# The keys' low parts of the attention logits as two zero-padded 128-row tiles in place of one tile read by halves

## The chip, the cores and the metric

The kernel runs on one core of a Trainium2 chip. The metric is the device time of one execution in microseconds (us), lower is better. The core has five engines that each run their own list of instructions in order: TensorE (PE in the profile, its weight loads as PEld), VectorE (DVE), ScalarE (ACT), GpSimd (POOL) and SyncE (SP), which here issues the transfers.

## What is computed

Two transformer layers, one after the other, on 512 tokens of width 1024 in float32. The first has sliding-window attention with a sink, differential attention and a convolutional feed-forward block. The second has sparse latent attention (an index score picks the keys), a gated linear recurrence and a merge of both. The change touches one kind of product, the logits of queries against keys in heads of 64, which the reference has in four places:

```python
HEAD_DIM = 64
# swa_sink_attention, WINDOW = 128: a block of 128 queries against 256 keys
scores = jnp.einsum("bnqhgd,bnkhd->bnhgqk", qb, kk).astype(jnp.float32)
scores = scores * (HEAD_DIM ** -0.5)
# diff_attention, Q_BLOCK = 128: 4 heads of 2 maps, against all earlier keys
s = jnp.einsum("bqhmd,bkhmd->bhmqk", q_blk, k).astype(jnp.float32)
# sparse_mla_attention: index scores of 8 heads, then the logits of 16 heads
s_idx = jax.nn.relu(jnp.einsum('btjd,bsd->btjs', qi.astype(f32), k_idx_f))
s_idx = jnp.einsum('btjs,btj->bts', s_idx, wi.astype(f32))
_, idx = lax.top_k(s_idx, topk)
logits = jnp.einsum('bthc,btkc->bthk', ql.astype(f32), c_sel)
```

## The kernel before

All activations lie transposed, features on the 128 partitions and the 512 tokens along the free dimension. A projection ("unit") is a 1024 x 128 piece of a weight matrix: eight contraction steps, and in each three matmuls of 512 columns, because every float32 operand is split into a high part (type fp32r, one pass through TensorE) and a low part that holds the rest: high times high, high times low, low times high (`mm3`, lines 534 to 546). The weights come by DMA into `wr`; ACT makes their high part `wh`, and POOL or DVE the low part `wl` (`hi_w`, `lo_w`, lines 477 to 511). Where the four `wh` buffers are taken, the two parts go into ordinary slots and are named `sh` and `sl`.

The logits take heads in pairs, e = 0 and 1, on partitions 0 to 63 and 64 to 127. The query tile `sq` of each e (`stack_q`, lines 614 to 631) holds the high part in its own 64 partitions and the low part in the other 64. The key tile `sk` of each e (`stack_k`, lines 633 to 647) holds the high part twice, so one matmul over 128 rows gives high times high plus low times high. What is left, query high times key low, comes from one more tile `skl`, whose lower half belongs to e = 0 and upper half to e = 1. `logits` (lines 649 to 659) issues four matmuls per block of 128 queries: two over 128 rows (`sk`) and two over 64 rows (`skl`), the latter on the upper and on the lower half of TensorE's array; the results are accumulated in two banks `ps_lg`. They have 256, 384 or 512 columns, by how many keys the block sees.

`stack_k` makes its tiles with two ACT copies (`sk`), two DVE copies of 64 partitions (`sk<-sk`, CAST in the profile) and two DVE subtractions (`skl`). It is called 14 times: once for the windowed keys (`ka`), four times for the differential keys (`kb0` to `kb3`), once for the index keys (`kn`) and eight times in the last attention stage, there straight from the bank in which the pair's keys were projected (`ev_q`, lines 1705 to 1719). `logits` is called 76 times: 32 in the first layer (47 to 177 us: 24 of 256 columns, 4 of 384, 4 of 512), 12 in the index scores (850 to 930 us: 4 of each width), 32 in the last attention stage (1040 to 1205 us: 16, 8 and 8).

The order of all instructions is settled while the program is built. The projections are issued in a fixed list, and between their contraction steps a planner (`sched`, lines 437 to 451) lets the other jobs, written as generators, emit their next piece as soon as its clock for each engine says that the inputs are there. `account` (lines 288 to 355) moves these clocks by a price per instruction. `vp` (lines 357 to 360) gives an elementwise job to POOL or to DVE, whichever clock is earlier. So an instruction added to one engine can move others:

```python
elif key == "P":
    c = 0.15 + n * 0.0021
p = max(self.free["P"], now) + PRM["pe"] + bias
return self.nc.gpsimd if p < max(self.free["D"], now) else self.nc.vector
```

Intermediate tiles come from one pool of 52 slots of 128 x 512 float32 (`slot`, line 266). A new tile waits for the last readers of the slot that it gets.

Of the kernel before, what the change touches and what calls it, by code (L numbers as in the profile page):

```python
# [12 lines left out]
F32 = mybir.dt.float32  # L13
F32R = mybir.dt.float32r
# [219 lines left out]
class _Build:  # L234
# [189 lines left out]
    def ok(self, g):  # L424
# [3 lines left out]
        if h == "T":  # L428
            return g.ready <= now + PRM["lt"]
        if h == "L":  # L430
            return self.cur >= UIDX[PRM["tk"]] and max(g.ready, self.free["D"]) <= now + PRM["ll"]
# [182 lines left out]
    def stack_q(self, src, scale=None):  # L614
        nc = self.nc
        A = [self.slot("sq0", F32R), self.slot("sq1", F32R)]
        R = (slice(0, 64), slice(64, 128))
        for e in range(2):
            yield "A"
            if scale is None:  # L620
                nc.scalar.activation(A[e][R[e], :], src[R[e], :], AF.Copy)
            else:
                nc.scalar.activation(A[e][R[e], :], src[R[e], :], AF.Identity, scale=scale[R[e], :])
        for e in range(2):
            yield "D"
            if scale is None:
                nc.vector.tensor_sub(A[e][R[1 - e], :], src[R[e], :], A[e][R[e], :].bitcast(F32))
                continue
            nc.vector.scalar_tensor_tensor(A[e][R[1 - e], :], src[R[e], :], scale[R[e], :],
                                           A[e][R[e], :].bitcast(F32), op0=OP.mult, op1=OP.subtract)  # L630
        return A

    def stack_k(self, src):
        nc = self.nc
        B = [self.slot("sk0", F32R), self.slot("sk1", F32R)]
        L = self.slot("skl", F32R)
        R = (slice(0, 64), slice(64, 128))
        for e in range(2):
            yield "A"
            nc.scalar.activation(B[e][R[e], :], src[R[e], :], AF.Copy)  # L640
        for e in range(2):
            yield "D"
            nc.vector.tensor_copy(B[e][R[1 - e], :], B[e][R[e], :])
        for e in range(2):
            yield "D"
            nc.vector.tensor_sub(L[R[e], :], src[R[e], :], B[e][R[e], :].bitcast(F32))
        return B, L

    def logits(self, pls, q, k, b, c0, c1, o=0):
        nc = self.nc  # L650
        if c1 - c0 < 256:
            c1 = c0 + 256
        B, L = k
        w = slice(b * P, (b + 1) * P)
        for e in range(2):
            nc.tensor.matmul(pls[e][:, o:o + c1 - c0], q[e][:, w], B[e][:, c0:c1], start=True, stop=False)
        for e in range(2):
            r = slice(64 * e, 64 * e + 64)
            nc.tensor.matmul(pls[e][:, o:o + c1 - c0], q[e][r, w], L[r, c0:c1], start=False, stop=True)

    def new_xs(self):
        out = []
# [157 lines left out]
    def block1(self):  # L820
# [68 lines left out]
        def swa(b):  # L889
# [3 lines left out]
            for gp in range(2):  # L893
# [3 lines left out]
                for g in (0, 1):  # L897
                    self.logits(pls, T[f"qa{2 * gp + g}"], T["ka"], b, c0, c0 + 256, g * 256)
                Lp = [self.slot("L"), self.slot("L")]
                for g in (0, 1):  # L900
# [1044 lines left out]
```

## Time and profile before

| | |
|---|---|
| three runs | 1345.79, 1349.64, 1350.53 us; median 1349.64 us |
| span of the profiled execution (first to last instruction) | 1344.5 us |
| PE busy | 1305.5 us, 97% of the span, 6748 matmuls |
| DVE, ACT, POOL busy | 903.1, 706.9, 286.8 us (67%, 53%, 21%) |
| bytes moved | 113.23 MB, mean 84 GB/s |

The page gives the profiled execution's span, and no time of its own beside it; the three runs are 1.3 to 6.0 us longer than that span, the median 5.1 us. A matmul's busy time is modelled and overlaps the next one's, so what a stretch costs PE is read from the starts of the instructions. Nearly every row has line 214, that of a helper which records each instruction; rows are told apart by the names of the tiles (output <- inputs), and "64\*128" beside a matmul means that it uses 64 of the array's 128 rows.

### The profile page before, as it was taken

How to read it: one execution, taken by the hardware profiler on the slowest of the kernel's cores; microseconds unless marked ns; L12 is line 12 of the kernel's file. 1: busy time of each engine (PE TensorE's matmuls, PEld its weight loads, DVE VectorE, ACT ScalarE, POOL GpSimd, SP SyncE). 2: the span in 40 equal slices, each digit the busy share in tenths (PEclk: the TensorE clock that was granted, in tenths of full speed). 3: DMA queues.
4: the chain of work that ended last, by engine and by line, in shares of the span. 5: the costliest groups of instructions: out<-in, count | busy, mean ns of one | idle time of the engine just before them, and what ended most of it. 6: DMA issues, size and time to landing. Idle time of an engine off the chain costs nothing.

```text
span 1344.5 us, 17797 instructions
## 1 busy us (share of the span) xinstructions
PE 1305.5 (97%) x6748; PEld 1052.4 (78%) x6748; DVE 903.1 (67%) x1586; ACT 706.9 (53%) x1256; POOL 286.8 (21%) x176
## 2 busy tenths in 40 slices
PE   9999998999999999999999888999999999999997
PEld 6778888788888888888887876777788777777886
DVE  6767768877266736673677698588989667653354
ACT  6488675443234323441335447778772777773232
POOL 3200014323033303430343353031220000000111
PEclk9999999999999999999999998999999999999999
DMA  6212231132323332223324310222233121112221
GB/s 231 79 33 63 63 126 48 63 94 94 98 90 94 94 110 83 90 95 110 94 82 138 126 48 1 94 78 78 79 99 105 48 63 48 51 52 89 97 74 63
DMA packets 34245, 113.23 MB, mean 84 GB/s; under 512 B 3824, under 2 KB 5872, under 8 KB 34160
## 3 DMA queue, kind: packets, MB, share of 16 engines
q1 hardware_dynamic: 32192, 109.48, 25.2%
q10 hardware_dynamic: 1968, 2.62, 0.6%
q8 instruction: 53, 0.87, 0.3%
q14 instruction: 32, 0.26, 0.1%
HBM read 109.99 MB, written 2.10 MB: 83 GB/s over the span
## 4 chain that ended last, share of the span: by engine, by line
PE 80%; DVE 12%; ACT 4%; issue 1%; DMA 1%; POOL 0%; ACTq 0%; SPq 0%; DVEq 0%; POOLq 0%
PE ps_mm L214 61%; PE ps_lg L214 9%; PE ps_o L214 8%; PE ps_pt L214 3%; DVE c L214 3%; DVE sl L214 1%; DVE xl L214 1%; DVE sq L214 1%; ACT c L214 1%; ACT wh L214 1%; ACT L214 1%; DVE yo L214 1%; DVE score L214 1%; DVE fs L214 0%; ACT sq L214 0%
## 5 line engine op out<-in xcount | busy, mean ns | idle before, releaser
L214 PE MATMUL ps_mm<-xh,wh 128*128 128x512 f32 x840 | 342.3, 408 | 1.2 <-ACT xh L214 0.7
L214 PE MATMUL ps_mm<-xh,wl 128*128 128x512 f32 x840 | 331.8, 395 | 0.6 <-POOL wl L214 0.6
L214 PE MATMUL ps_mm<-xl,wh 128*128 128x512 f32 x840 | 331.7, 395 | 0.0
L214 POOL TENSOR_TENSOR wl<-wr,wh 128x1024 fp32r<-128x1024 f32 (+1 forms) x69 | 164.1, 2379 | 535.4 <-ACT wh L214 473.7
L214 ACT ACTIVATE wh<-wr 128x1024 fp32r<-128x1024 f32 (+1 forms) x179 | 185.1, 1037 | 133.4 <-PE ps_mm L214 98.5
L214 DVE SCALAR_TENSOR_TENSOR c<-u,vec,c 128x511 f32<-128x511 f32 (+1 forms) x128 | 171.6, 1342 | 74.6 <-ACT c L214 72.3
L214 PEld LDWEIGHTS ps_mm<-xh,wh 128*128 128x128 f32 x840 | 158.5, 189 | 44.6 <-issue 5.7
L214 PEld LDWEIGHTS ps_mm<-xh,wl 128*128 128x128 f32 x840 | 158.3, 188 | 39.1 <-POOL wl L214 1.1
L214 PEld LDWEIGHTS ps_mm<-xl,wh 128*128 128x128 f32 x840 | 158.5, 189 | 33.8 <-DVE xl L214 0.5
L214 DVE TENSOR_TENSOR wl<-wr,wh 128x1024 fp32r<-128x1024 f32 (+1 forms) x110 | 132.6, 1206 | 70.5 <-ACT wh L214 69.8
L214 PE MATMUL ps_mm<-acth,wh 128*128 128x512 f32 x216 | 84.9, 393 | 2.3 <-DVE fs L214 2.3
L214 PE MATMUL ps_mm<-actl,wh 128*128 128x512 f32 x216 | 84.8, 392 | 0.0
L214 PE MATMUL ps_mm<-acth,wl 128*128 128x512 f32 x216 | 84.6, 392 | 0.0
L214 ACT ACT_TABLE_LOAD x63 | 80.8, 1283 | 4.3 <-PE ps_mm L214 2.3
L214 ACT ACTIVATE acth<-c 128x512 fp32r<-128x512 f32 x32 | 20.2, 632 | 113.9 <-DVE c L214 111.1
L214 ACT ACTIVATE c<-c 128x512 f32<-128x512 f32 x32 | 20.2, 632 | 81.7 <-DVE c L214 81.7
L214 ACT ACTIVATE c<-u,vec 128x512 f32<-128x512 f32 x64 | 51.5, 808 | 13.4 <-DVE u L214 13.4
L214 POOL TENSOR_TENSOR sq<-sq,sq 128x256 f32<-128x256 f32 (+1 forms) x36 | 33.8, 938 | 90.2 <-ACT sq L214 74.2
L214 POOL TENSOR_TENSOR mxl<-g,mxh 128x512 fp32r<-128x512 f32 x8 | 12.3, 1533 | 189.5 <-ACT mxh L214 189.5
L214 DVE TENSOR_TENSOR u<-ps_mm,rbn 128x512 f32<-128x512 f32 (+1 forms) x63 | 42.5, 676 | 15.1 <-PE ps_mm L214 15.1
L214 PEld LDWEIGHTS ps_mm<-acth,wh 128*128 128x128 f32 x216 | 40.8, 189 | 11.5 <-DVE fs L214 2.7
L214 PEld LDWEIGHTS ps_mm<-acth,wl 128*128 128x128 f32 x216 | 41.0, 190 | 8.6
(406 smaller groups left out, 2608.9 us busy)
## 6 DMA issues: line engine op xcount, KB each, us to landing
wr<-in_wpk_dram SPq DMA_DIRECT2D x197, 512.0 KB, 3.5
xres<-in_xt_dram SPq DMA_DIRECT2D x8, 256.0 KB, 5.4
wr<-in_wpk_dram SPq DMA_DIRECT2D x6, 256.0 KB, 5.5
wrg<-in_wrg_dram ACTq DMA_DIRECT2D x4, 256.0 KB, 3.7
out_dram<-o SPq DMA_DIRECT2D x4, 256.0 KB, 2.2
out_dram<-o ACTq DMA_DIRECT2D x3, 256.0 KB, 2.3
con<-in_con_dram SPq DMA_DIRECT2D x1, 576.0 KB, 6.1
wuv<-in_wukv_dram ACTq DMA_DIRECT2D x2, 256.0 KB, 5.1
```

The lines of the kernel that those rows point to most:

```text
L214: r = f(*a, **k)
```

## The change

`stack_k` keeps the low part in two tiles, `skl0` and `skl1`, each with its own 64 partitions filled as before and the other 64 set to zero by a POOL memset (28 in all). `logits` then multiplies the whole query tile of each e with the whole low tile: four matmuls over 128 rows. The added half of each product is query low times zero.

```diff
     def stack_k(self, src):
         nc = self.nc
         B = [self.slot("sk0", F32R), self.slot("sk1", F32R)]
-        L = self.slot("skl", F32R)
+        L = [self.slot("skl0", F32R), self.slot("skl1", F32R)]
         R = (slice(0, 64), slice(64, 128))
+        for e in range(2):
+            nc.gpsimd.memset(L[e][R[1 - e], :].bitcast(F32), 0.0)
         for e in range(2):
             yield "A"
             nc.scalar.activation(B[e][R[e], :], src[R[e], :], AF.Copy)
...
         for e in range(2):
             yield "D"
-            nc.vector.tensor_sub(L[R[e], :], src[R[e], :], B[e][R[e], :].bitcast(F32))
+            nc.vector.tensor_sub(L[e][R[e], :], src[R[e], :], B[e][R[e], :].bitcast(F32))
         return B, L
...
-        B, L = k
         w = slice(b * P, (b + 1) * P)
-        for e in range(2):
-            nc.tensor.matmul(pls[e][:, o:o + c1 - c0], q[e][:, w], B[e][:, c0:c1], start=True, stop=False)
-        for e in range(2):
-            r = slice(64 * e, 64 * e + 64)
-            nc.tensor.matmul(pls[e][:, o:o + c1 - c0], q[e][r, w], L[r, c0:c1], start=False, stop=True)
+        for n, K in enumerate(k):
+            for e in range(2):
+                nc.tensor.matmul(pls[e][:, o:o + c1 - c0], q[e][:, w], K[e][:, c0:c1], start=n == 0, stop=n == 1)
```

The order of the instructions moves with it in some stretches. On PE the first logits of the third pair in the last attention stage stood like this before; the rows are output bank <- moving tile, stationary tile, and the size of the result:

```order
L214 MATMUL ps_mm_9541<-xh_7060,wh_9245 128x512
L214 MATMUL ps_mm_9541<-xl_7061,wh_9245 128x512
L214 MATMUL ps_mm_9541<-xh_7060,wl_9250 128x512
L214 MATMUL ps_lg_9548<-sk_1506_9487,sq_1489_9395 128x512
L214 MATMUL ps_lg_9549<-sk_1507_9488,sq_1490_9396 128x512
L214 MATMUL ps_lg_9548<-skl_9489,sq_1489_9395 128x512
L214 MATMUL ps_lg_9549<-skl_9489,sq_1490_9396 128x512
L214 MATMUL ps_mm_9541<-xh_7084,wh_9245 128x512
L214 MATMUL ps_mm_9541<-xl_7085,wh_9245 128x512
```

and stand like this now:

```order
L214 MATMUL ps_o_9487<-PTm_9530,V_7364 64x128
L214 MATMUL ps_o_9487<-PTm_9545,V_7364 64x128
L214 MATMUL ps_lg_9568<-sk_1514_9511,sq_1497_9419 128x512
L214 MATMUL ps_lg_9569<-sk_1515_9512,sq_1498_9420 128x512
L214 MATMUL ps_lg_9568<-skl_1516_9513,sq_1497_9419 128x512
L214 MATMUL ps_lg_9569<-skl_1517_9514,sq_1498_9420 128x512
L214 MATMUL ps_mm_9579<-xh_7075,wh_9266 128x512
L214 MATMUL ps_mm_9579<-xl_7076,wh_9266 128x512
```

The group has the same four matmuls, now on two low tiles; what moved is the first contraction step of a projection, which stood ahead of it and now stands behind it.

On POOL the rows from the end of the start-up to the first feed-forward weights were:

```order
L214 TENSOR_TENSOR sq_150<-sq_150,sq_244 128x512
L214 TENSOR_TENSOR wl_368<-wr_265,wh_358 128x1024
L214 TENSOR_TENSOR wl_439<-wr_318,wh_437 128x1024
L214 TENSOR_TENSOR wl_569<-wr_427,wh_557 128x1024
L214 TENSOR_TENSOR wl_679<-wr_441,wh_653 128x1024
L214 TENSOR_TENSOR sl_1312<-wr_681,sh_1306 128x512
L214 TENSOR_TENSOR wl_1827<-wr_1575,wh_1797 128x1024
```

and are, as far as the memsets of the second differential head:

```order
L214 TENSOR_TENSOR sq_150<-sq_150,sq_244 128x512
L214 MEMSET skl_52_357 64x512
L214 MEMSET skl_53_358 64x512
L214 TENSOR_TENSOR wl_371<-wr_265,wh_361 128x1024
L214 TENSOR_TENSOR wl_429<-wr_294,wh_418 128x1024
L214 MEMSET skl_92_571 64x512
L214 MEMSET skl_93_572 64x512
L214 TENSOR_TENSOR wl_575<-wr_431,wh_560 128x1024
L214 TENSOR_TENSOR wl_685<-wr_456,wh_659 128x1024
L214 MEMSET skl_169_936 64x512
L214 MEMSET skl_170_937 64x512
```

The memsets stand between the same jobs on weights; of those one changed places with DVE (the job on `wr_294`, here `wl_429`, was on DVE before; the job on `wr_318`, there `wl_439`, is on DVE now).

In the last attention stage POOL had nothing but one job on weights:

```order
L214 TENSOR_TENSOR wkl_8663<-wuk_8634,wkh_8662 128x512
L214 TENSOR_TENSOR g_8493<-g_8493,h_8649 128x512
L214 TENSOR_TENSOR sl_8741<-wr_8660,sh_8726 128x512
L214 TENSOR_TENSOR wl_9567<-wr_9252,wh_9560 128x1024
L214 TENSOR_TENSOR mxl_10950<-g_10747,mxh_10949 128x512
```

It now has the 16 memsets of the eight pairs, of which the last ten stand here:

```order
L214 MEMSET skl_1569_9705 64x512
L214 MEMSET skl_1570_9706 64x512
L214 MEMSET skl_1637_9979 64x512
L214 MEMSET skl_1638_9980 64x512
L214 MEMSET skl_1687_10193 64x512
L214 MEMSET skl_1688_10194 64x512
L214 MEMSET skl_1746_10415 64x512
L214 MEMSET skl_1747_10416 64x512
L214 TENSOR_TENSOR wl_10612<-wr_10351,wh_10597 128x1024
L214 MEMSET skl_1800_10637 64x512
L214 MEMSET skl_1801_10638 64x512
L214 TENSOR_TENSOR mxl_10992<-g_10795,mxh_10991 128x512
```

Only the last pair's memsets stand behind another job; the others follow each other, each pair's two together.

## Rows read from the trace of the kernel before

**Rows 1.** The page, busy time by engine, and shares of the chain that ended last.

```profile
PE 1305.5 (97%) x6748; PEld 1052.4 (78%) x6748; DVE 903.1 (67%) x1586; ACT 706.9 (53%) x1256; POOL 286.8 (21%) x176
...
PE 80%; DVE 12%; ACT 4%; issue 1%; DMA 1%; POOL 0%; ACTq 0%; SPq 0%; DVEq 0%; POOLq 0%
```

**Rows 2.** Busy by stretch: length; PE, PEld, DVE, ACT, POOL; PE clock; DMA.

```profile
47.00:177.00 130.00, 129.87 (x965) 107.21 (x966) 91.89 (x292) 96.53 (x255) 8.45 (x4) 1.00 0.17 54
850.00:930.00 80.00, 79.47 (x343) 60.67 (x342) 56.54 (x75) 63.69 (x91) 14.89 (x7) 1.00 0.20 66
930.00:990.00 60.00, 58.96 (x252) 46.89 (x251) 58.46 (x105) 49.01 (x61) 8.10 (x4) 1.00 0.28 88
...
1040.00:1205.00 165.00, 165.00 (x976) 120.66 (x975) 109.44 (x295) 125.22 (x262) 2.42 (x1) 1.00 0.17 52
```

**Rows 3.** PE in order of time, 1045 to 1052 us: start, length, operation, rows*columns.

```profile
1045.25 0.62 PE L214 MATMUL ps_lg<-sk,sq 128*128 128x512 f32 x2
1045.81 0.50 PE L214 MATMUL ps_lg<-skl,sq 64*128 64x512 f32 x2
1046.24 0.50 PE L214 MATMUL ps_mm<-xh,wh 128*128 128x512 f32 x1
1046.58 0.40 PE L214 MATMUL ps_mm<-xl,wh 128*128 128x512 f32 x1
...
1048.45 0.52 PE L214 MATMUL ps_lg<-sk,sq 128*128 128x384 f32 x2
1048.89 0.45 PE L214 MATMUL ps_lg<-skl,sq 64*128 64x384 f32 x2
1049.27 0.51 PE L214 MATMUL ps_mm<-xh,wh 128*128 128x512 f32 x1
1049.61 0.40 PE L214 MATMUL ps_mm<-xl,wh 128*128 128x512 f32 x1
...
1050.78 0.40 PE L214 MATMUL ps_lg<-sk,sq 128*128 128x256 f32 x2
1051.11 0.38 PE L214 MATMUL ps_lg<-skl,sq 64*128 64x256 f32 x2
1051.43 0.50 PE L214 MATMUL ps_mm<-xh,wh 128*128 128x512 f32 x1
1051.77 0.40 PE L214 MATMUL ps_mm<-xl,wh 128*128 128x512 f32 x1
```

**Rows 4.** The chain in order of time: 256-wide matmuls at 204 us, 512-wide at 1021 us.

```profile
204.10 4.32 PE ps_lg L214 x36
...
1021.94 19.28 PE ps_mm L214 x84
```

**Rows 5.** Instructions on the logits banks: count, ns min/median/max, first and last start, forms.

```profile
L214 PE MATMUL ps_lg<-sk,sq x152: 276/336/501, 48.1 to 1203.7; 128*128 128x256 f32 x88, 128*128 128x512 f32 x32, 128*128 128x384 f32 x32
...
L214 PE MATMUL ps_lg<-skl,sq x152: 379/382/502, 48.5 to 1203.9; 64*128 64x256 f32 x88, 64*128 64x512 f32 x32, 64*128 64x384 f32 x32
```

**Rows 6.** All engines in order of time: the last pair's keys and its first logits.

```profile
1188.38 0.88 DVE L214 CAST sk<-sk 64x512 fp32r<-64x512 f32 x2
1189.27 1.39 DVE L214 TENSOR_TENSOR skl<-ps_lg,sk 64x512 fp32r<-64x512 f32 x2
...
1191.85 0.73 PE L214 MATMUL ps_lg<-sk,sq 128*128 128x512 f32 x2
```

**Rows 7.** Groups on POOL by shape: count | busy us, mean ns | idle before.

```profile
L214 POOL TENSOR_TENSOR sl<-wr,sh 128x512 fp32r<-128x512 f32 x9 | 14.7, 1647 | 76.9 <-ACT sh L214 45.0 <-DVE sl L214 31.8
...
L214 POOL TENSOR_TENSOR wl<-wr,wh 128x512 fp32r<-128x512 f32 x2 | 2.6, 1298 | 9.6 <-ACT wh L214 9.6
...
L1936 POOL MEMSET const-float32-0.0<- 128x1 f32 x1 | 0.1, 99 | 0.2 <-issue 0.2
```

**Rows 8.** POOL in order of time at 64 us, one job on weights.

```profile
64.36 2.37 POOL L214 TENSOR_TENSOR wl<-wr,wh 128x1024 fp32r<-128x1024 f32 x1 [6.21 <-PE ps_pt L214]
```

**Rows 9.** DVE in order of time at the same moment.

```profile
64.38 2.64 DVE L214 CAST sk<-sk 64x512 fp32r<-64x512 f32 x1
```

## The prediction

> **What bounds the kernel now.** I read the page first: PE is busy for 97% of the span, and 80% of the chain that ended last is PE work [rows 1]. A busy PE is an overlapping, modelled time, so the share alone does not say that every nanosecond taken off PE counts. The second view is the busy time by stretch, for the three stretches that hold logits [rows 2]. In 47 to 177 us and in 1040 to 1205 us PE is busy for 129.87 of 130 and 165.00 of 165 us, while DVE has 91.89 and 109.44, ACT 96.53 and 125.22, and POOL 8.45 and 2.42. There PE sets the pace and the other engines have 24% of their time or more left. In 850 to 930 us PE is also full, but the stretch behind it, 930 to 990 us, is one in which DVE is busy for 58.46 of 60 us. A PE that arrives there earlier may meet a DVE that is not ready.
>
> The third view is PE in order of time around one group of logits of each width [rows 3]. The reader is to look at starts, not lengths. A plain stream has two rhythms: 36 matmuls of 256 columns in 4.32 us, 0.120 us each, and 84 of 512 columns in 19.28 us, 0.230 us each [rows 4]. For 384 columns I take the middle, 0.175 us. In the groups of logits the rhythm breaks at the 64-row pair. With 256 columns, the two full matmuls start at 1050.78, the pair of 64 rows at 1051.11, the next projection at 1051.43 and the one after it at 1051.77. So the full pair takes 0.33 us until the narrow pair starts (two plain ones: 0.24), the narrow pair 0.32 us, and even the first projection behind it 0.34 us instead of 0.23.
>
> The narrow pair itself is cheap: the two together occupy 0.38 us, and one alone 0.382 us at the median [rows 3, 5], so they run side by side. What is dear is getting into and out of the narrow form.
>
> **The change, part by part.** *The matmuls.* Each group keeps four, all over 128 rows. I price the new group as four plain matmuls of its width plus one plain projection (0.23), and compare it with the old one from the first full matmul to the second projection:
>
> - 256 columns: before 1051.77 - 1050.78 = 0.99 us; after 4 x 0.120 + 0.23 = 0.71; saved 0.28.
> - 384 columns: before 1049.61 - 1048.45 = 1.16 us; after 4 x 0.175 + 0.23 = 0.93; saved 0.23.
> - 512 columns: before 1046.58 - 1045.25 = 1.33 us; after 5 x 0.23 = 1.15; saved 0.18.
>
> There are 152 narrow matmuls, 88 of 256, 32 of 384 and 32 of 512 columns [rows 5], two per group, so 44, 16 and 16 groups. Saved: 44 x 0.28 + 16 x 0.23 + 16 x 0.18 = 12.3 + 3.7 + 2.9 = 18.9 us. Where another group or a transpose stands behind the pair the gain differs by some hundredths. By stage: 24, 4 and 4 groups in the first layer give 8.4 us, four of each in the index scores 2.8, and 16, 8 and 8 in the last stage 7.8.
>
> *What of it reaches the end.* In the first layer and in the last stage I count all of it, since PE is full there. In the index scores I count half of 2.8 us: DVE at 58.46 of 60 us [rows 2] speaks for losing it all, the 1.5 us in which even there DVE is idle for keeping part. Lost 1.4 us, bounds 0 and 2.8.
>
> *The memsets.* 28 on POOL, 64 partitions x 512 elements. The trace has none of that size. The nearest rows are the one-element memset, 0.10 us, and a two-input POOL job of 512 elements, 1.30 to 1.65 us [rows 7]. The memset has the element count of the latter but reads nothing, so I take 1.3 us as its price, and 0.1 as the lower end. That makes 36 us of POOL time, 8 x 2 x 1.3 = 21 us of it in the last stage, where POOL has 162 us to spare, and 13 us in the first layer, where it has 121. POOL takes its list in order: a job on weights behind a pair of memsets starts up to 2.6 us later, and that costs nothing as long as the weights are wanted a unit (24 matmuls x 0.23 = 5.5 us) or more later. SP's list of transfers is as long as before. What waits for a memset is PE, at the first `skl` of a new key: it is issued with the ACT copies, and behind those stand two DVE copies (0.88 us) and two subtractions (1.39) [rows 6], so 2.6 us of memsets are covered, if they start when the copies do. If they start late, by a slot whose last reader is late, they appear on PE.
>
> A memset can also hold up a DVE copy. At 64.38 us one copy of 64 x 512 took 2.64 us, where two take 0.88 elsewhere; it began 0.02 us behind a POOL job of 2.37 us and ended with it [rows 6, 8, 9]. The Trainium skill ("SBUF — State Buffer", Who interferes with whom) says that GpSimd and a DVE copy in its two-port mode exclude each other for a whole instruction, and the copy at 64.38 us agrees. For the last pair the subtractions end at 1190.66 and the logits start at 1191.85 us [rows 6], a gap of 1.19 us. One copy held for one memset costs PE 1.3 - 1.19 = 0.11 us, in eight pairs 0.9 us. I take 1 us; the lower end is 0, the upper is a rival below.
>
> *The moved order.* POOL and DVE swap a few jobs, and PE's list differs at the end of the first layer, in the index scores and in the last stage. Nothing is added there, PE is full on both sides, and the feed-forward block, 500 us, keeps its order. I take 0, with 2 us either way.
>
> *Sum.* Against the span of 1344.5 us: -18.9 + 1.4 + 1 = -16.5, so 1328.0 us. The shown median is 5.1 us longer than the span; with that the median becomes **1333.1 us**.
>
> **The rivals.** *Half of it is given back.* Faster PE stretches make other chains end last. In the last stage ACT would be busy for 125 of 157 us instead of 165, and DVE for 109. For it: the order was laid out with its jobs close together, as the gap of 1.19 us shows. Against it: PE never waits in 165 us. At half of 18.9 us the time is 1340.2 us.
>
> *The memsets hold the keys up.* If both copies of a pair are held for a whole memset each, the keys come 2.6 to 3.3 us later, and PE stands for 1.4 to 2.1 us in each of the eight last pairs: 11 to 17 us. For it: the copy at 64.38 us. Against it: POOL is idle there, so the memsets can run before the copies do. With 14 us and the index scores' 1.4 the gain is 3.5 us: 1346.1 us.
>
> *Side by side is worth more than the breaks cost: slower.* Two narrow matmuls that share the array take the time of one; the change makes them two. If the breaks of 0.09 us before and 0.2 and 0.1 us behind the pair do not come from the narrow form but stay (with the change of the key tile, say, or of the bank), then each group gains one plain matmul: 44 x 0.120 + 16 x 0.175 + 16 x 0.23 = 11.8 us, and the time is 1361.4 us. For it: the pair is indeed side by side. Against it: the plain 256-wide stream goes over several banks and weights and keeps 0.120 us [rows 4], so neither makes a break by itself. The point from which it decides: the breaks sum to 0.40 us with 256 columns and to 0.41 with 512, against 0.12 and 0.23 for the extra matmul; slower needs less than that to go away. The Trainium skill ("TensorEngine Tiling (Array Packing)", Theoretical Speedup) promises up to twofold for a contraction of 64 or less by this very packing; by that alone the change would cost those 11.8 us. The same page (Tiling Modes, Key Properties) has a change of tiling mode drain the array, and the breaks in the trace agree.
>
> **How the numbers follow.** The measurement can tell about 0.5%, 6.7 us, from no change: 1342.9 to 1356.4 us. My forecast has a chance of 0.70; its own range is 1328 (all 18.9 us and 2 more) to 1338. Half given back 0.13, the memsets 0.12, slower 0.05. Faster: 0.70 + 0.13 = 0.83; no change: 0.12; slower: 0.05. The range goes from 1327, the lower end with a little of the scatter of the shown runs, to 1346, which takes in the first rival and about half of the second; left out are the third, the rest of the second and the ends, not quite 2 in 10.
>
> **What would show each step.** In the profile of the changed kernel the second pair of every group should start two plain rhythms behind the first pair, 0.24 us with 256 columns, each of its matmuls a rhythm apart, and the second projection behind it should come after 0.23 us. The stretch of the last stage should be some 7 us shorter, with PE still full. Memsets should take 1.3 us or less, and no row of PE's waits should name POOL and `skl`. I am wrong if the second pair keeps starting 0.3 us or more behind the first, if PE waits for DVE's copies or POOL in the last stage for more than 3 us in all, or if the saving up to 177 us is gone by 250 us.

## The result, and the profile after

The change makes the kernel faster. Five runs give 1329.96 to 1336.2 us, median 1331.37 us, against 1349.64 us (1345.79 to 1351.13 in five runs) before: a ratio of 0.9884, 95% interval 0.987 to 0.9899, or 18.3 us by the medians. The prediction was 1333.1 us. The profiled execution took 1329.96 us and its span is 1328.1 us, 16.4 us shorter than the span before; the forecast of the span was 1328.0. Of all the runs below only one is slow: in the second experiment, 1436.54 us at a granted clock of 0.85 where the others have 0.99; its median of 1348.48 us counts it, and the nine others have 1348.14.

The page of the changed kernel, the same two lines as [rows 1]:

```profile
PE 1290.4 (97%) x6748; PEld 1065.6 (80%) x6748; DVE 901.3 (68%) x1586; ACT 708.0 (53%) x1258; POOL 301.8 (23%) x204
...
PE 76%; DVE 16%; ACT 4%; issue 2%; DMA 1%; SPq 0%; POOL 0%; ACTq 0%; DVEq 0%; POOLq 0%
```

PE has as many matmuls as before and is busy for 15.1 us less; POOL has 28 instructions and 15.0 us more. That alone says little. The starts in order of time say more. The same three places as in [rows 3], one for each width, in the timeline of PE (start, length, operation, rows\*columns):

```profile
1037.20 0.62 PE L214 MATMUL ps_lg<-sk,sq 128*128 128x512 f32 x2
1037.66 0.63 PE L214 MATMUL ps_lg<-skl,sq 128*128 128x512 f32 x2
1038.13 0.39 PE L214 MATMUL ps_mm<-xh,wh 128*128 128x512 f32 x1
1038.36 0.40 PE L214 MATMUL ps_mm<-xl,wh 128*128 128x512 f32 x1
...
1040.23 0.52 PE L214 MATMUL ps_lg<-sk,sq 128*128 128x384 f32 x2
1040.59 0.51 PE L214 MATMUL ps_lg<-skl,sq 128*128 128x384 f32 x2
1040.94 0.39 PE L214 MATMUL ps_mm<-xh,wh 128*128 128x512 f32 x1
1041.16 0.40 PE L214 MATMUL ps_mm<-xl,wh 128*128 128x512 f32 x1
...
1042.33 0.40 PE L214 MATMUL ps_lg<-sk,sq 128*128 128x256 f32 x2
1042.57 0.40 PE L214 MATMUL ps_lg<-skl,sq 128*128 128x256 f32 x2
1042.81 0.39 PE L214 MATMUL ps_mm<-xh,wh 128*128 128x512 f32 x1
1043.04 0.39 PE L214 MATMUL ps_mm<-xl,wh 128*128 128x512 f32 x1
```

From the first pair of logits to the second projection this is 1.16, 0.93 and 0.71 us for 512, 384 and 256 columns, where [rows 3] have 1.33, 1.16 and 0.99. The breaks are gone: with 256 columns 0.24, 0.24 and 0.23 us stand where 0.33, 0.32 and 0.34 stood. The reader is to see that the second pair's own line did not get shorter (0.40 us against 0.38): what fell is the distance to the next start.

The windows, as in [rows 2] (length; PE, PEld, DVE, ACT, POOL with their counts; PE clock; DMA):

```profile
47.00:177.00 130.00, 128.93 (x996) 114.10 (x995) 95.83 (x303) 101.32 (x268) 13.15 (x11) 1.00 0.19 58
850.00:930.00 80.00, 80.00 (x357) 65.41 (x356) 61.89 (x85) 67.93 (x97) 15.52 (x7) 1.00 0.24 73
930.00:990.00 60.00, 58.31 (x251) 46.57 (x250) 56.23 (x98) 47.80 (x59) 14.22 (x6) 1.00 0.27 85
1040.00:1205.00 165.00, 165.00 (x1043) 131.39 (x1042) 109.76 (x295) 126.45 (x272) 8.63 (x13) 1.00 0.18 55
```

PE is still full in the last attention stage and does 1043 matmuls in the time of 976. In the first layer it now has 1.07 us of idle time in 130, where it had 0.13.

Where the 16.4 us lie is read from marks that both traces have. The third column is worked out from the starts of the 76 groups: from each group's first full matmul to the second instruction behind the group, summed; where two groups stand right behind each other, the stretch that both would claim is counted once.

| stretch | before to after, us | in the groups alone | forecast |
|---|---|---|---|
| up to the first logits | 48.13 to 47.60, -0.5 | | 0 |
| first logits to the first layer's last | 121.69 to 115.07, -6.6 | 31.38 to 24.21, -7.2 | -8.4 |
| from there to the first index logits | 682.83 to 683.42, +0.6 | | 0 |
| first index logits to the first product of the recurrence's output (`hxh`) | 136.47 to 134.96, -1.5 | 13.85 to 11.11, -2.7 | -1.4 |
| from there to the last stage's first logits | 56.13 to 56.15, 0.0 | | 0 |
| first logits there to the first product of the last projection (`mxh`) | 243.56 to 234.96, -8.6 | 36.78 to 28.68, -8.1 | -6.8 |
| from there to the end | 55.74 to 55.98, +0.2 | | 0 |

The groups alone give 18.0 us; 18.9 were forecast. The first row is scatter: over the nine profiles on record the first logits start between 47.5 and 49.6 us, in both forms. And with the moved order the second, third and fourth stretch do not hold the same matmuls as before: 915 for 918, 3188 for 3191 and 582 for 576. At 0.23 us for each, the three are -5.9, +1.3 and -2.9 us when the same work is counted.

The memsets, in the groups of POOL by shape (count | busy us, mean ns | idle before), the line to hold beside [rows 7]:

```profile
L214 POOL MEMSET skl<- 64x512 f32 x28 | 14.7, 526 | 147.4 <-PE ps_pt L214 62.7 <-DVE m L214 22.8 <-DVE skl L214 19.8
```

One takes 0.53 us, not 1.3. PE's waits have no line that names POOL and `skl`; the only one on POOL is 0.5 us for a `sq`. Between 1030 and 1200 us PE has no wait at all.

### The profile page after: what moved, and what is told of

It reads as the page before. It is cut to its first block, busy times and chain, and to the rows that moved or that the text cites. A ratio compares the mean times of both kernels' runs of the same rounds, so it can differ in the third digit from the quotient of the medians.

```text
span 1328.1 us, 17863 instructions
## 1 busy us (share of the span) xinstructions
PE 1290.4 (97%) x6748; PEld 1065.6 (80%) x6748; DVE 901.3 (68%) x1586; ACT 708.0 (53%) x1258; POOL 301.8 (23%) x204
## 4 chain that ended last, share of the span: by engine, by line
PE 76%; DVE 16%; ACT 4%; issue 2%; DMA 1%; SPq 0%; POOL 0%; ACTq 0%; DVEq 0%; POOLq 0%
PE ps_mm L214 58%; PE ps_lg L214 8%; PE ps_o L214 8%; DVE c L214 3%; PE ps_pt L214 3%; DVE sq L214 1%; DVE xl L214 1%; DVE sl L214 1%; DVE score L214 1%; ACT wh L214 1%; ACT c L214 1%; DVE wl L214 1%; DVE yo L214 1%; DVE m L214 1%; ACT L214 1%
## 5 line engine op out<-in xcount | busy, mean ns | idle before, releaser
L214 PE MATMUL ps_mm<-xh,wh 128*128 128x512 f32 x840 | 336.8, 401 | 0.0
L214 DVE TENSOR_TENSOR u<-ps_mm,rbn 128x512 f32<-128x512 f32 (+1 forms) x63 | 42.5, 676 | 15.1 <-PE ps_mm L214 15.1
L214 POOL MEMSET skl<- 64x512 f32 x28 | 14.7, 526 | 147.4 <-PE ps_pt L214 62.7
L214 PEld LDWEIGHTS ps_mm<-actl,wh 128*128 128x128 f32 x216 | 40.5, 188 | 8.4
```

The source lines that it names most:

```text
L214: r = f(*a, **k)
```

## Experiments

The theory: changing between 128-row and 64-row matmuls costs PE about 0.4 us per group, and the change saves just that; the memsets and the moved order are worth little. Against it stand three others: that the gain comes from the new order of the instructions; that the break belongs to two narrow matmuls running side by side, or to the key tile, and not to the change of form; and that the memsets eat a part of the gain. Four runs below were timed beside one set of runs of the kernel before (median 1347.97 us), the other three beside another (1346.81 us).

### The wide form in the old order

The changed kernel, but the memsets move none of the planner's clocks and both low tiles count as one, so that every engine has its instructions in the order of the kernel before, the memsets aside.

```diff
+        ALIAS[L[1].name] = L[0].name
         for e in range(2):
-            nc.gpsimd.memset(L[e][R[1 - e], :].bitcast(F32), 0.0)
+            self.realnc.gpsimd.memset(L[e][R[1 - e], :].bitcast(F32), 0.0)
```

> The wide form alone: two zero-padded low tiles and four matmuls over 128 rows, as in the change, but every instruction of every engine stands where it stood in the kernel before (the planner is told nothing of the memsets). Theory, the form on TensorE: 13 to 19 us less than before (ratio 0.986 to 0.990), the groups of logits in the plain rhythm of 0.12, 0.175 and 0.23 us. Rival, the moved order made the gain: within 5 us of before (ratio 0.996 to 1.004), although the rhythm is plain.

Measured: median 1333.03 us, ratio 0.989 (0.9871 to 0.9908), span 1330.5 us, 14.0 below that of before. The form alone carries the gain. The last stage (the table's sixth row) is 236.19 us, 7.4 shorter than before, and its groups are shorter by the same 7.4 us (36.78 to 29.35). What is missing against the changed kernel is 1.2 us there and the whole gain of the index stage, which takes 137.0 us (136.47 before), although its groups are shorter by 2.7 us. The window behind the index scores, in the same columns as above:

```profile
930.00:990.00 60.00, 58.31 (x244) 46.37 (x243) 55.90 (x96) 47.50 (x59) 13.09 (x6) 0.97 0.25 81
```

The granted clock is 0.97 here and 1.00 in the changed kernel, and PE does 244 matmuls where the changed kernel does 251. The lower clock is worth up to 1.8 us (an estimate: 0.03 of 60 us); another 1.7 us are PE's waits, shown below under "The index scores". Of the two totals, the intervals overlap: this run and the changed kernel can't be told apart.

### The new order with narrow low products

The changed kernel with its tiles, memsets and order, but each low product only over its own 64 rows.

```diff
-        for n, K in enumerate(k):
-            for e in range(2):
-                nc.tensor.matmul(pls[e][:, o:o + c1 - c0], q[e][:, w], K[e][:, c0:c1], start=n == 0, stop=n == 1)
+        B, L = k
+        for e in range(2):
+            nc.tensor.matmul(pls[e][:, o:o + c1 - c0], q[e][:, w], B[e][:, c0:c1], start=True, stop=False)
+        for e in range(2):
+            r = slice(64 * e, 64 * e + 64)
+            nc.tensor.matmul(pls[e][:, o:o + c1 - c0], q[e][r, w], L[e][r, c0:c1], start=False, stop=True)
```

> The new order alone: tiles, memsets and the order of all engines as in the changed kernel, but the low products use 64 rows again, side by side. Theory: the gain is gone, within 4 us of before (ratio 0.997 to 1.003), with breaks of 0.2 to 0.4 us around each narrow pair. Rival, the moved order made the gain: 10 to 18 us less than before.

Measured: median 1348.48 us, ratio 0.9999 (0.999 to 1.0009), span 1346.3 us. Order, tiles and memsets alone give nothing. The timeline of PE has the breaks back, on separate key tiles:

```profile
1054.11 0.40 PE L214 MATMUL ps_lg<-sk,sq 128*128 128x256 f32 x2
1054.44 0.38 PE L214 MATMUL ps_lg<-skl,sq 64*128 64x256 f32 x2
1054.76 0.50 PE L214 MATMUL ps_mm<-xh,wh 128*128 128x512 f32 x1
1055.10 0.39 PE L214 MATMUL ps_mm<-xl,wh 128*128 128x512 f32 x1
```

0.33, 0.32 and 0.34 us, as in [rows 3]; so the shared key tile is not what breaks the rhythm. The order is not worth quite nothing everywhere: the last stage takes 241.95 us, 1.6 less than before, while up to the first index logits 2.7 us are lost, 1.3 of them between the last attention projection and the first down projection, where the granted clock is lower (last section). The index stage takes 137.11 us with its 582 matmuls, against 136.47 with 576 before.

### The 512-column narrow pair cut in two

The kernel before, with each 512-column pair of 64 rows as two pairs of 256 columns. Sixteen groups get two more narrow matmuls, but no further change of form.

```diff
+        h = 256 if c1 - c0 == 512 else c1 - c0
+        for a in range(c0, c1, h):
+            for e in range(2):
+                r = slice(64 * e, 64 * e + 64)
+                self.realnc.tensor.matmul(pls[e][:, o + a - c0:o + a - c0 + h], q[e][r, w], L[r, a:a + h], start=False, stop=a + h == c1)
```

> The kernel before, with the narrow pair of each of the 16 groups of 512 columns cut into two pairs of 256 columns, one behind the other; nothing else moves. Theory, the price is that of changing between the forms: the second pair starts 0.11 to 0.13 us behind the first, and the time moves by less than 1 us. Rival, each narrow matmul or pair pays its own break: the second pair starts 0.2 us or more behind the first and the 16 groups cost 2 to 5 us more in all, seen in the starts (the medians can hardly tell it).

Measured: median 1346.82 us, ratio 1.0 (0.999 to 1.001), span 1345.2 us. The timeline, where x4 are the four narrow ones:

```profile
1087.18 0.62 PE L214 MATMUL ps_lg<-sk,sq 128*128 128x512 f32 x2
1087.74 0.50 PE L661 MATMUL ps_lg<-skl,sq 64*128 64x256 f32 x4
1088.17 0.51 PE L214 MATMUL ps_mm<-xh,wh 128*128 128x512 f32 x1
1088.51 0.39 PE L214 MATMUL ps_mm<-xl,wh 128*128 128x512 f32 x1
```

From the first narrow start to the projection it is 0.43 us, as for the uncut pair (1045.81 to 1046.24 in [rows 3]). So a further narrow pair within the narrow form costs no further break. Where inside the 0.43 us the second pair starts was a miss: 0.22 us behind the first and not one plain rhythm. By width the stretch from narrow start to projection is 0.32, 0.38 and 0.43 us in [rows 3], 0.11 us more for 256 columns more; a fixed 0.21 us is left. Part of that fixed time seems to appear between the two pairs here and behind the pair otherwise. That is a reading of the sums; no run shows where inside TensorE it is spent.

### One narrow low product

The changed kernel, with the low product of e = 0 over 64 rows and that of e = 1 over 128. No narrow matmul has a partner to run beside.

```diff
+            r = slice(0, 64 if e == 0 else P)
+            nc.tensor.matmul(pls[e][:, o:o + c1 - c0], q[e][r, w], L[e][r, c0:c1], start=False, stop=True)
```

> The changed kernel, with the low product of the first head of each pair back on 64 rows and that of the second over 128 rows. Theory: the change of form is paid in full and the side-by-side pair is lost, so this is the slowest of all: per group 0.11, 0.17 and 0.23 us more than before (256, 384, 512 columns), 11 us more than before and 29 more than the changed kernel, about 1360 us (1354 to 1364). Rival, the breaks come from two matmuls meeting in different rows of the array: without a partner there is none, and the time stays near the changed kernel, 1329 to 1338 us.

Measured: median 1361.24 us, ratio 1.0094 (1.0075 to 1.0114), span 1361.2 us: slower than both kernels. The timeline (the row of `skl` joins the narrow matmul and the full one behind it):

```profile
1063.85 0.39 PE L214 MATMUL ps_lg<-sk,sq 128*128 128x256 f32 x2
1064.18 0.70 PE L214 MATMUL ps_lg<-skl,sq 64*128 64x256 f32 x2
1064.71 0.40 PE L214 MATMUL ps_mm<-xh,wh 128*128 128x512 f32 x1
1064.95 0.40 PE L214 MATMUL ps_mm<-xl,wh 128*128 128x512 f32 x1
```

0.33 us up to the narrow matmul, as with a pair; then 0.31 us from it to the full one behind it, and 0.22 us from that to the projection. One narrow matmul holds the array as long as a pair does, so the pair does run side by side, and the break needs no partner: it is the change of form. Half the narrow work gives all of the break. The Trainium skill ("TensorEngine Tiling (Array Packing)", Key Properties) says that a change of the tiling mode drains the engine; the 0.33 and 0.31 us agree, in place of 0.24 and 0.12.

The groups account for 10.9 us of the 16.7 us by which the span grew (the same sum as in the table). The rest lies around them, 3.4 us of it between the last down projection and the first index logits, where the granted clock over 765 to 850 us is 0.86 and was 0.94 before; what causes that part is open.

### Four memsets for one

The changed kernel, each memset issued four times, three of them outside the planner's clocks.

```diff
             nc.gpsimd.memset(L[e][R[1 - e], :].bitcast(F32), 0.0)
+            for _ in range(3):
+                self.realnc.gpsimd.memset(L[e][R[1 - e], :].bitcast(F32), 0.0)
```

> The changed kernel with every memset issued four times, one behind the other, all else in its place: 84 more memsets of 0.52 us, 44 us more on POOL. Theory, POOL's idle time hides them: within 4 us of the changed kernel (1328 to 1336 us), PE's waits for POOL under 1 us. Rival, memsets hold the keys or DVE's copies up: four memsets for each of two tiles are 4.2 us against some 3.5 us from the key's projection to its logits, so PE would stand 1 us or more in most of the last eight pairs, 8 us or more in all (1339 us and above).

Measured: median 1335.19 us, ratio 0.9912 (0.9897 to 0.9927), span 1331.7 us, 3.5 above that of the changed kernel. The groups on POOL and the window of the last stage:

```profile
L641 POOL MEMSET skl<- 64x512 f32 x84 | 44.8, 534 | 4.8
L214 POOL MEMSET skl<- 64x512 f32 x28 | 14.7, 526 | 123.7 <-PE ps_pt L214 53.5 <-PE ps_o L214 36.9 <-PE ps_mm L214 15.6
```

```profile
1040.00:1205.00 165.00, 165.00 (x1043) 131.32 (x1042) 112.21 (x298) 129.21 (x275) 28.23 (x49) 1.00 0.18 56
```

44.8 us more of POOL time. In the last stage, which has the most memsets, PE stays full with the same 1043 matmuls, and the stage is 235.00 us against 234.96. So 2.1 us of memsets per tile are covered there, and the single ones of 0.53 us all the more. Four DVE copies grew from 0.42 to between 0.55 and 0.83 us, and PE stood for none of them. Of the 3.5 us, 1.9 lie between the last down projection and the first index logits (88.35 us in the changed kernel, 90.26 here), and 0.6 ahead of the first logits, which is within the scatter. In the first of these the granted clock over 765 to 850 us is 0.90, and 0.92 in the changed kernel, which is worth up to 1.7 us (an estimate: 0.02 of 85 us), so the memsets are not shown to cost anything there. One wait of PE, 0.6 us, names POOL's `wl`; the seventh experiment, with single memsets, has the same one.

### A third order

The wide form with the memsets outside the planner's clocks and the low tiles counted apart, which gives an order that is neither that of before nor that of the change.

```diff
-            nc.gpsimd.memset(L[e][R[1 - e], :].bitcast(F32), 0.0)
+            self.realnc.gpsimd.memset(L[e][R[1 - e], :].bitcast(F32), 0.0)
```

> The wide form in a third order, which comes out when the planner is told of two low tiles but not of their memsets; no instruction is added or left out against the changed kernel. Theory, the form makes the gain and the order moves a few us at most: 1328 to 1337 us (ratio to before 0.986 to 0.992). Rival, the order of the changed kernel was a lucky one: 1340 us or more.

Measured: median 1332.6 us, ratio 0.9901 (0.9876 to 0.9926), span 1330.4 us. With the first experiment there are three orders of the wide form, with medians of 1331.37, 1332.6 and 1333.03 us and intervals that overlap. The medians lie within 1.7 us of each other; what the order is worth isn't settled by these runs.

### The index scores narrow again

The changed kernel, with the 12 groups of the index scores back on 64 rows.

```diff
-    def logits(self, pls, q, k, b, c0, c1, o=0):
+    def logits(self, pls, q, k, b, c0, c1, o=0, narrow=False):
...
+                r = slice(64 * e, 64 * e + 64) if n == 1 and narrow else slice(0, P)
```

> The changed kernel in its own order, with the 12 groups of the index scores back on 64 rows. By the starts on PE those 12 groups cost 2.8 us more. If half of that had been lost behind them, as predicted, the time is 1.4 us longer than the changed kernel; if DVE paces everything there, 0; if PE does, 2.8. To be read from the start of the recurrent block's projection (wr) against the first index group, since the medians scatter by more.

Measured: median 1334.45 us, ratio 0.991 (0.9891 to 0.993), span 1331.4 us. The index stage takes 137.11 us, 2.15 more than in the changed kernel, of the 2.7 us that its groups are shorter. So in this order the wide form keeps most of its gain there. The 0.6 us that are missing are one wait of PE, for ACT's `xch`, which is 0.80 us here and 1.46 us in the changed kernel.

## Why the prediction was right

**The bound.** It was right that PE sets the pace and that starts have to be read. The last stage shows it best: PE is full on both sides, and in the first experiment, in an unchanged order, the stage became shorter by the 7.4 us by which its groups did. None of the signs of being wrong appeared: the second pair starts 0.24 us behind the first, PE has no wait in the last stage, and the saving of the first layer is not gone by 250 us (the last product of the attention projection starts at 209.25 us, before at 216.07).

**The price of a group.** 0.28, 0.23 and 0.18 us were forecast, and the rows give 0.28, 0.23 and 0.17. The explanation behind them also held: getting into the narrow form and out of it is what costs (experiments two, three and four), and the pair itself is cheap. With the fixed 0.21 us of the third experiment, a group of 256 columns before had breaks of 0.09, 0.21 and 0.11 us, 0.41 in all; the one extra pass that the wide form needs costs 0.12.

**The first layer was sized too high**: -8.4 us forecast, -7.2 in the groups, -6.6 in the stage (-5.9 with the same matmuls; -6.9 in the order of before, in the first experiment). The step that failed is "I count all of it, since PE is full there", together with one price for all neighbours. Of the 1.2 us in the groups, 0.7 are in three places (at 67.54, 107.30 and 149.79 us). At the last two PE, earlier now, gets late to its second logits matmul (0.24 us of waiting for DVE's `sq` at 149.79 us; at 107.30 no wait is recorded). At the first a product stands behind the logits that has a narrow form of its own, 64 of the array's columns (128\*64), as the timeline of the changed kernel shows:

```profile
68.58 0.40 PE L214 MATMUL ps_lg<-skl,sq 128*128 128x256 f32 x2
68.91 0.28 PE L214 MATMUL ps_o<-va,PT 128*64 128x64 f32 x2
```

From the last pair of logits to it there are 0.33 us and not 0.24, so a break of 0.09 stays there; and the 0.11 of a projection behind the pair was not there to be saved. Of the rest of the 1.2 us, 0.25 are in five groups behind which a transpose stands and not a projection (0.165 us became 0.109, a gain of 0.06 where I had 0.11); and 0.2 in the first 16, which saved 0.267 each where nothing else intervened, and not 0.28. Outside the groups, PE waits 0.64 us for DVE's `m` ahead of the group at 67.54 us, where it waited 0.14 before. A stage with 0.13 us of idle time before has no room to show how near its other engines are.

**The index scores**: half of 2.8 was a choice between bounds. The stage gives -1.5 us, with -2.7 in its groups, and that this is so close to -1.4 is luck: the stage now holds six projection matmuls, 1.4 us, that stood ahead of it before. What remained varied from order to order (1.5, 1.0 in the third and, in the first experiment, less than nothing). What was lost can be read from PE's waits in the timeline, for `relu`, with which ACT empties the banks of the index scores, and for `xch`, the high part of the recurrent branch's input. Before:

```profile
895.65 0.50 PE L214 MATMUL ps_lg<-xch,wgh 128*128 128x512 f32 x1 [0.54 <-ACT relu L214]
...
968.25 0.49 PE L214 MATMUL ps_lg<-xch,wgh 128*128 128x512 f32 x1 [0.81 <-ACT xch L214]
```

in the first experiment:

```profile
887.63 0.50 PE L214 MATMUL ps_lg<-xch,wgh 128*128 128x512 f32 x1 [1.55 <-ACT relu L214]
...
959.78 0.50 PE L214 MATMUL ps_lg<-xch,wgh 128*128 128x512 f32 x1 [1.46 <-ACT xch L214]
```

and in the changed kernel, where only the second is left:

```profile
960.19 0.50 PE L214 MATMUL ps_lg<-xch,wgh 128*128 128x512 f32 x1 [1.46 <-ACT xch L214]
```

In the order of before the two waits grew by 1.7 us, of the 2.7 that the groups gave; in the third order they are 1.55 and 1.46 as well. In the changed kernel one grew by 0.65. The engine named is ACT, but behind it stands DVE, in the timelines of ACT and of DVE:

```profile
957.08 0.63 ACT L214 ACTIVATE hxh<-g 128x512 fp32r<-128x512 f32 x1 [5.43 <-DVE g L214]
...
959.52 0.62 ACT L214 ACTIVATE xch<-xrc 128x512 fp32r<-128x512 f32 x1
```

```profile
958.88 0.73 DVE L214 SCALAR_TENSOR_TENSOR xrc<-ps_mm,vec,xrc 128x509 f32<-128x509 f32 x1
```

ACT had waited 5.43 us for DVE's `g` ahead of the rows that end in `xch`, and the `xrc` that `xch` reads is finished by DVE at 959.61 us, after rows without a gap from 952 us on. So the reason given, a DVE that is nearly full, holds at this place; the half did not follow from it.

**The memsets** were priced at 1.3 us from a POOL job that reads two inputs; they took 0.53. The 1 us for held copies came to nothing that PE could feel. All engines around the last pair's keys, in order of time, to be held beside [rows 6]:

```profile
1170.31 1.09 POOL L214 MEMSET skl<- 64x512 f32 x2
...
1171.54 0.42 DVE L214 CAST sk<-sk 64x512 fp32r<-64x512 f32 x1 [0.63 <-ACT sk L214]
...
1173.57 0.42 DVE L214 CAST sk<-sk 64x512 fp32r<-64x512 f32 x1 [1.61 <-ACT sk L214]
...
1174.01 1.39 DVE L214 TENSOR_TENSOR skl<-ps_lg,sk 64x512 fp32r<-64x512 f32 x2
...
1175.82 0.63 PE L214 MATMUL ps_lg<-sk,sq 128*128 128x512 f32 x2
```

The memsets are over at 1171.40, before the first copy begins: POOL is idle there and runs ahead, as the case against the second rival had it. The gap between the subtractions' end and the logits is now 0.42 us, where it was 1.19, so a held copy would be felt more today than before. The one copy that was held before [rows 9] is held again, in the timelines of DVE and of POOL:

```profile
61.76 2.58 DVE L214 CAST sk<-sk 64x512 fp32r<-64x512 f32 x1
```

```profile
61.67 2.38 POOL L214 TENSOR_TENSOR wl<-wr,wh 128x1024 fp32r<-128x1024 f32 x1 [5.03 <-ACT wh L214]
```

It is held by a job on weights, not by a memset. It ends at 64.34 us, 0.29 us behind the POOL job; so it was before (67.02 and 66.73 us), where the prediction had it end with the job. The Trainium skill ("SBUF — State Buffer", Who interferes with whom) has GpSimd and such a copy exclude each other; this pair of rows agrees again, and in no pair of the last stage did it reach PE.

**The moved order**, 0 with 2 us either way: in the last stage it gave 1.2 us (against the first experiment) to 1.6 (second against before), so the last stage's -8.6 is -7.4 for the form and -1.2 for the order. Elsewhere it seems to take some of that back, but there the granted clock differs from profile to profile too. The near agreement of the totals, -16.4 and -16.5 us, is therefore partly luck: the first layer fell short by 1.8 us, the last stage gave 1.8 more.

**From span to run.** I added 5.1 us to the span. Each profiled execution here is 1.8 us longer than its span (1329.96 and 1328.1; 1332.28 and 1330.5); the rest was the scatter of the first three runs. The changed kernel's median is 3.3 us above its profiled span, and that makes the difference between 1333.1 and 1331.37.

**The rivals.** "Half given back" falls: 18.0 us in the groups became 16.4, of which 1.2 come from the order in the last stage. "The memsets hold the keys up" falls with the fifth experiment. "Side by side is worth more" falls as well: the pair does run side by side, but its breaks go with the narrow form. The Trainium skill's up to twofold ("TensorEngine Tiling (Array Packing)", Theoretical Speedup) is not met in this kernel, where the packed pair stands alone between full matmuls: the packing saves 0.12 to 0.23 us per group and costs 0.41.

## What to carry to other kernels

Before packing two 64-row matmuls side by side, look in the timeline at the starts before, in and behind the pair, not at its length: here one visit to the narrow form costs 0.41 us whatever its width, and it saves one plain matmul of its width. By these numbers (0.23 us per 512 columns) a visit has to carry about 900 columns per matmul to pay for itself, all pairs in it counted (an estimate; no run here had such a visit); with less, fill the other half with zeros and stay in the full form. Let an engine that is idle write the zeros, and see that it can do so ahead of the job that waits.

## What the runs showed of the hardware that was not expected

A memset of 64 x 512 float32 on POOL takes 0.53 us, less than half of the nearest POOL job on 512 elements (1.30 us).

A single narrow matmul pays the same 0.31 us as a pair until the next full one starts, and a second narrow pair starts 0.22 us behind the first while the sum stays 0.43.

The granted clock fell in a place where it had not. Two windows of the changed kernel, between the attention and the feed-forward block of the first layer:

```profile
210.00:215.00 5.00, 2.53 (x28) 2.35 (x27) 5.00 (x9) 3.39 (x9) 3.48 (x5) 1.00 0.00 2
215.00:220.00 5.00, 5.00 (x32) 5.00 (x31) 4.02 (x13) 2.42 (x7) 2.27 (x4) 0.66 0.00 0
```

PE, full up to 210 us, is busy for 2.53 of 5 us there while DVE is full; then the clock is at 0.66 over the next 5 us, a part of them at 1.2 GHz in place of 2.4. Over 175 to 250 us it is 0.95, before it was 1.00, and from the last attention projection to the first down projection it takes 1.3 us longer. The kernel before has similar idle places (PE at 3.42 of 5 us in 215 to 220) without the fall. The experiment in the new order with narrow products also shows 0.95, and the one with the cut pairs, whose order is that of before, 0.98. So the wide form isn't needed for it; what decides it is open. Such falls also differ between profiles of one order: over 175 to 250 us it is 0.98 in the fifth experiment, whose order is that of the changed kernel. And the kernel before has one that the changed kernel has not, 0.83 over 730 to 740 us; from the first to the last down projection it takes 437.51 us, the changed kernel 436.29. So the table's third row says little about the change.
